# First two columns of each weight group run abreast in the scan stage of a two-layer encoder

## Chip, cores and metric

One Trainium2 chip, one core. The metric is the device time of one execution in microseconds. TensorE is called PE here, VectorE DVE, ScalarE ACT, GpSimd POOL and SyncE SP, as in the profile.

## The reference

Two token sequences of 512 x 1024 (s = 0 and s = 1) go through the same two layers. Layer 0 is an RWKV-7 mixer that scans forward and backward; layer 1 is attention in a 2-D neighbourhood.

```python
def _rwkv7_branch(xn, mu, w_r, w_k, w_v, w_z, ...):
    ...
    lerp = lambda j: xn + xx * mu[j]
    r = heads(lerp(0) @ w_r)
    k = heads(lerp(1) @ w_k)
    v = heads(lerp(2) @ w_v)
    z = xn @ w_z
    ...
    for d in range(2):
        ...                       # decay, a, k_d by two small products each
        ys.append(_wkv7_scan(r, decay, k_d, v, -kk, kk * a, reverse=(d == 1)))
    ...                           # y: sum of both, normed by head, plus a bonus
    return (y * silu(z)) @ w_o

def _natten_branch(xn, w_in, b_in, rpb, w_o, b_o):
    q, k, v, z = jnp.split(xn @ w_in + b_in, 4, axis=-1)
    ...                           # windowed softmax attention with a bias
    return (o * silu(z)) @ w_o + b_o

def _trunk(x, ...):
    for i in range(2):
        h = branch_i(_rms_norm(x, pre_norm_g[i]))
        x = x + _rms_norm(h, post_norm_g[i])
    return x
```

## The kernel before

**Products.** Every large product is split in two halves of lower precision: an fp32 block becomes a high half (`hi`, an ACT cast, lines 745 for weights and 771 for inputs) and a low half (`lo`, a DVE subtraction, lines 747 and 773). A *column* is one 128-wide slice of outputs for all 512 tokens: eight blocks of channels (k = 0 to 7), and for each a *triple* of matmuls (lines 826 to 828: hi x hi, hi x lo, lo x hi), all added up in one PSUM bank (`pm`). The weights of a column come in two halves of 512 columns (`raw`, `whi`, `wlo`; three raw buffers, four split ones).

**Stages.** `prelude` (to about 170 us) norms the inputs and makes the first columns. `scan_phase` (to about 1170 us) runs the scan of all heads, and beside it 80 columns. `rest` does the attention; its columns are made by `gemm` (lines 430 to 432).

**The scan stage.** Eight pairs of heads' blocks (four for each sequence) go through `prep` (lora products, lines 896 and 897, with `th` on ACT, line 900), `inverse` (elimination on DVE, lines 1018 and 1020, between transposes at lines 1011, 1028 and 1033; then four takes of a `pm` bank, copied by lines 1056 and 1059), eight `step`s each (lines 1186 to 1254), and `finish` (lines 1279 to 1317), which writes y. PSUM has three `pm` banks in this stage, one `us`, and two each of `pf` and `zy`.

**The columns beside it.** They come in groups that share one input: group 0 is w_r of s = 0, 1 w_v of s = 0, 2 w_k, 3 w_r, 4 w_v of s = 1 (8 columns each), 5 six columns of w_z of s = 1, 6 w_o of s = 0 (8, whose input is y of the first four finishes), 7 the other two of w_z, and 8 the first 24 columns of w_in of s = 0. At most nine pairs of input halves fit (`NACT` = 18), so a block of the next group can only be made when the last column of the group before has used one up. `flow` (line 722) holds the generators: `loads` and `splits` for weights, `fetched` and `operands` for inputs, `products` for the triples, and `posts` for what follows a column (its *end*: copy, activation, store, for v also two transposes that take a `pm` bank each). In group 8 inputs are made by `residual`, `scaled` and `squares`, and the ends wait for the norm of that input, which takes `pm` banks in `rstds`.

**The order** of PE, DVE and ACT in this stage is fixed when the kernel is built. `weave` (line 1617 on) keeps a clock model and asks generators (*threads*) for what they can do next; each has a rank, and the lowest that can start goes first. PE work goes only when no other engine's does. Steps have rank 0, `prep` 1.5, ends 2, `operands` 2.5, `splits` 3 or 9 (9 when more than one split half is in stock), `inverse` 5, `products` 9. Where the model finds nothing for PE and the clock might drop, it puts a warming matmul (line 1643) into a spare part of the `zy` bank. `inverse` is one thread: it takes the eight one after another.

Before the change a column runs k = 0 to 7 before the next begins, and two threads of ends take columns in turn: `posts(0)` the even ones, `posts(1)` the odd ones.

Of the kernel before, what the change touches and what calls it, by code (L numbers as in the profile page):

```python
# [19 lines left out]
P = 128  # L20
T = 512
D = 1024
KT = D // P
NP = 8
NCH = 8
# [25 lines left out]
class Clock:  # L51
# [40 lines left out]
    def room(self, key, bufs):  # L92
        s = self.slots.get(key, ())
        return 0.0 if len(s) < bufs else min(self.left(n) for n in s)
# [137 lines left out]
class Trunk:  # L232
# [9 lines left out]
    TOK = True  # L242
    LAST = ("pg", "pg", "po", "pm")
    PG, PT, NK, NPT = 2, 2, 2, 3
    AHEAD, AHEADW, SCAN_A, SCAN_W = 0, 0, 300, 300
    NAB, NX, NR, NY, NSB, NBI = 2, 2, 2, 2, 4, 2
    NAK, NZ = 1, 1
# [25 lines left out]
    def name(self, s):  # L273
        self.uid += 1
        return f"{s}_{self.uid}"
# [356 lines left out]
    def column(self, s, kind, p, ps):  # L632

        nc, sp = self.nc, self.sp
        vt, act = nc.vector, nc.scalar
        first = lambda e: (e, None, lambda c, n=ps.tensor.name: c.at([n]))
        keep, whole = self.clock.keep, ps.tensor.name
        if kind == "z":

            o, th = self.tmp(), self.tmp()  # L640
            if s == 0:
                yield first("D")
                vt.tensor_tensor(o, ps, self.rstd0, op=ALU.mult)
                ps = o
            yield "A" if s == 0 else first("A")
            keep.add(whole)
            act.activation(th, ps, AF.Tanh, scale=0.5)
            yield "D"
            keep.discard(whole)
            vt.scalar_tensor_tensor(o, th, 1.0, ps, op0=ALU.add, op1=ALU.mult)  # L650
            self.save("z", s, p, o)
            return
        yield "A", None, lambda c: max(c.at([ps.tensor.name]), min(c.room(("tmp", id(self.main)), self.NTMP), 1e10))
        o = self.tmp()
        if kind == "k":
            keep.add(whole)
        act.copy(o, ps)
        self.save(kind, s, p, o)
        if kind == "r":
            self.made.add((kind, s, p))  # L660
            return
        if kind == "k":
            yield "A"
            keep.discard(whole)
            sq = self.tmp()
            act.activation(sq, ps, AF.Square, scale=self.vec("kk", p))
            free, room = self.bank()
            yield "P", free, lambda c: max(room(c), c.at([sq.tensor.name]))
            ss = self.p("pm", (2, T))
            nc.tensor.matmul(ss, self.ssel, sq, start=True, stop=True)  # L670
            yield "A"
            row = self.tmp((2, T))
            act.copy(row, ss)
            if p == 0:
                sp["ss", s] = self.dram(f"ss{s}", (16, T))
            self.load(sp["ss", s][2 * p:2 * p + 2], row)
            self.made.add((kind, s, p))
            if p == NP - 1:
                yield "S", None, lambda c: c.at([sp["ss", s].tensor.name])

                rn = self.tmp((P, 64))
                self.load(rn, sp["ss", s].rearrange("a (b c) -> (a b) c", b=8))
                yield "A"
                act.activation(rn, rn, AF.Sqrt)
                yield "D"
                vt.tensor_scalar(rn, rn, 1e-12, None, op0=ALU.max)
                vt.reciprocal(rn, rn)
                sp["rn", s, 0] = self.dram(f"rn{s}", (16, T))
                self.load(sp["rn", s, 0].rearrange("a (b c) -> (a b) c", b=8), rn)
                self.made.add(("rn", s))  # L690
            return

        if p == 0:

            sp["vt", s] = self.dram(f"vt{s}", (4, 2, NCH // 2, 2, L, 2, 2, HD))
        yield "A"
        back = self.tmp()
# [14 lines left out]
        self.made.add((kind, s, p))  # L712
# [9 lines left out]
    def flow(self):  # L722


        nc, did, ck = self.nc, self.did, self.clock
# [5 lines left out]
        for k, t in enumerate(self.groups[0][1]):  # L731
            x[0, k] = t

        def loads():
            for c, (_, _, src, _) in enumerate(cols):
                for j in range(2):
                    yield "S", lambda: did["load"] < did["split"] + self.NRAW
                    raw[2 * c + j] = self.load(self.t("raw", (P, self.WP), self.NRAW), src[:, j * self.WP:(j + 1) * self.WP])
                    did["load"] += 1

        def splits():
            for h in range(2 * len(cols)):
                yield "A", lambda: h < did["load"] and h < did["k"] // 4 + self.NW, lambda c: c.at(name(raw[h]))
                hi, lo = (self.t(tag, (P, self.WP), self.NW, F32R) for tag in ("whi", "wlo"))
                nc.scalar.copy(hi, raw[h])  # L745
                yield "D"
                nc.vector.tensor_tensor(lo, raw.pop(h), hi.bitcast(F32), op=ALU.subtract)  # L747
                w[h] = hi, lo
                did["split"] += 1
# [63 lines left out]

        def products():
            free, room = self.bank()
            for c, (g, j, _, done) in enumerate(cols):
                for k in range(KT):
                    h = 2 * c + k // 4
                    at = slice(k % 4 * P, k % 4 * P + P)
                    yield (  # L820
                        "P", lambda: h in w and (g, k) in x and (k > 0 or (free() and c - 2 not in self.post)),
                        lambda c: max(c.at(name(*w[h], *x[g, k])), 0.0 if k else room(c)))
                    if k == 0:
                        ps = self.p("pm")
                    (hi, lo), (xh, xl) = w[h], x[g, k]
                    nc.tensor.matmul(ps, hi[:, at], xh, start=(k == 0), stop=False)  # L826
                    nc.tensor.matmul(ps, hi[:, at], xl, start=False, stop=False)  # L827
                    nc.tensor.matmul(ps, lo[:, at], xh, start=False, stop=(k == KT - 1))  # L828
                    did["k"] += 1
                    if j == len(self.groups[g][2]) - 1:  # L830
                        did["x"] += 1
                self.post[c] = done(ps)

        def posts(a):
            for c in range(a, len(cols), 2):
                yield "A", lambda: c in self.post
                yield from self.post[c]
                del self.post[c]
# [2 lines left out]
        return [  # L841
            Thread(lambda: 0, loads()), Thread(lambda: 3 if few() else 9, splits()), Thread(lambda: 0, fetched()), Thread(lambda: 2.5, operands()),
            Thread(lambda: 0.6, residual()), Thread(lambda: 0.6, scaled()), Thread(lambda: 0.6, squares()),
            Thread(lambda: 9, products()), Thread(lambda: 2, posts(0)), Thread(lambda: 2, posts(1))]


    def prep(self, s, p):
# [479 lines left out]
    def out0s(self, s, p, ps):  # L1327

        nc = self.nc
# [12 lines left out]
        else:  # L1342
# [1 line left out]
            nc.scalar.activation(sq, h, AF.Square)  # L1344
            yield "D"
            nc.vector.tensor_tensor(self.h_acc, sq, self.h_acc, op=ALU.add)
        if p == NP - 1:
            self.made.add(("h", s))

    def out0(self, s):  # L1350
# [307 lines left out]
    def scan_phase(self, mid):  # L1658
# [27 lines left out]
        def fetch():  # L1686
            for q in qs:
                st = self.steps[q]
                yield (
                    "S", lambda: did["states"] >= q - 1 and did["preps"] > st.n and ("v", st.s, 2 * st.pb + 1) in self.made,  # L1690
                    lambda c: c.at([self.sp["ab", st.s, st.pb].tensor.name]))
                self.fetch(st)
                did["fetch"] += 1
# [19 lines left out]

        def finish():
            for n, (s, pb) in enumerate(self.todo):
                yield "S", lambda: did["steps"] >= NCH * (n + 1) and ("z", s, 2 * pb + 1) in self.sp
                yield from self.finish(s, pb, self.steps[NCH * n].y)
                did["finish"] += 1

# [212 lines left out]
```

## Time and profile before

| | |
|---|---|
| time, median of 3 runs | 1655.09 us (1649.51 to 1655.29) |
| profiled execution | 1656.04 us, its span 1654.2 us |
| granted PE clock, mean | 0.977 |
| busy in the span | PE 94%, DVE 74%, ACT 61%, POOL 11% |
| scan stage | 170 to 1170 us of the span |
| prelude, `rest` | 0 to 170 us, 1170 to 1654.2 us |

Inversions, by the start of line 1011 on DVE and of the last copy (line 1059, an ACT pair of 1.2 us), and the first column of the groups, from its first triple to its end; all in us:

| inversion | starts | last copies | group | first column |
|---|---|---|---|---|
| 0 | 242.1 | 322.4 | 1 | 230.8 to 246.4 |
| 1 | 323.2 | 430.3 | 2 | 328.0 to 349.6 |
| 2 | 431.1 | 545.5 | 3 | 446.2 to 466.0 |
| 3 | 546.3 | 657.4 | 4 | 530.0 to 544.0 |
| 4 | 656.2 | 762.1 | 5 | 642.2 to 658.9 |
| 5 | 762.1 | 895.0 | 6 | 742.4 to 767.4 |
| 6 | 895.5 | 1021.4 | 7 | 850.2 to 871.7 |
| 7 | 1021.4 | 1092.0 | 8 | 877.0 to 921.6 |

The page gives each engine's busy time as a share of the span; a group's row gives its line, engine, operation and tiles, the count, then busy time in us and the mean of one in ns, then the idle time before it and what ended that. A row of the timeline gives the start, the time taken, and in brackets the idle time before it. A row of the windows gives the window, its length, and for each engine the busy time and the count.

### The profile page before, as it was taken

What the parts mean: (1) busy time and instruction counts of PE and PEld (TensorE: products, weight loads), DVE (VectorE), ACT (ScalarE), POOL (GpSimd) and SP (SyncE); (2) the same over time, 40 slices, a digit from 0 to 9 for tenths busy, and PEclk for the clock granted to TensorE, in tenths of its full rate; (3) what the DMA queues carried; (4) which work ended last, traced back from release to release, by engine and by line L of the source; (5) the groups of instructions that cost most, each with busy time, mean ns of one, the idle gap of its engine ahead of it and who ended that gap; (6) DMA issues with size and microseconds to landing.
All of it is one profiled execution on the core that took longest, in us unless ns stands there. A gap on an engine that the chain in (4) does not pass through costs nothing.

```text
span 1654.2 us, 46534 instructions
## 1 busy us (share of the span) xinstructions
PE 1558.4 (94%) x18826; PEld 1195.2 (72%) x18826; DVE 1220.0 (74%) x2711; ACT 1014.5 (61%) x2027; POOL 178.2 (11%) x338
## 2 busy tenths in 40 slices
PE   7989899898989998999888999999999999999998
PEld 6867667676767776766666777777777788777776
DVE  8886669588778786897788897855576685665564
ACT  6577655766755767566475665454567665455562
POOL 0000213311101133100000011000000002100000
PEclk9989999899999999999997999999999999999999
DMA  6455678666677687675776674554864346745553
GB/s 212 158 176 185 183 270 279 217 227 227 206 246 255 201 279 261 201 252 165 226 229 225 199 255 166 179 190 127 276 222 164 109 140 213 244 157 175 169 159 107
DMA packets 176184, 336.29 MB, mean 203 GB/s; under 512 B 20928, under 2 KB 53824, under 8 KB 175968
## 3 DMA queue, kind: packets, MB, share of 16 engines
q1 hardware_dynamic: 152480, 253.07, 47.7%
q0 software_dynamic: 23488, 80.23, 13.8%
q8 instruction: 148, 2.42, 0.6%
q14 instruction: 68, 0.56, 0.1%
HBM read 227.71 MB, written 105.51 MB: 201 GB/s over the span
## 4 chain that ended last, share of the span: by engine, by line
PE 48%; DVE 7%; ACT 5%; DMA 3%; issue 3%; POOL 0%; SPq 0%; DVEq 0%; ACTq 0%; POOLq 0%
PE pg L430 6%; PE pg L431 6%; PE pg L432 6%; PE pm L826 4%; PE pm L827 3%; PE pm L828 3%; PE pf L1114 2%; PE sc L1452 2%; PE po L1485 2%; PE pt L1470 2%; PE us L1233 1%; PE zy L1186 1%; PE us L1213 1%; PE zy L1237 1%; DMA v<-dv 1%
## 5 line engine op out<-in xcount | busy, mean ns | idle before, releaser
L826 PE MATMUL pm<-act,whi 128*128 128x512 f32 x640 | 283.9, 444 | 7.8 <-ACT act L795 3.2
L827 PE MATMUL pm<-act,whi 128*128 128x512 f32 x640 | 257.2, 402 | 10.8 <-DVE act L773 10.1
L828 PE MATMUL pm<-act,wlo 128*128 128x512 f32 x640 | 256.2, 400 | 5.5 <-DVE wlo L747 5.5
L430 PE MATMUL pg<-act,whi 128*128 128x512 f32 x384 | 158.4, 412 | 0.4 <-DVE tmp L1408 0.4
L826 PEld LDWEIGHTS pm<-act,whi 128*128 128x128 f32 x640 | 121.7, 190 | 50.9 <-issue 10.7
L379 ACT CAST whi<-raw 128x512 fp32r<-128x512 f32 x148 | 91.4, 617 | 107.7 <-PE pg L431 66.1
L432 PE MATMUL pg<-act,wlo 128*128 128x512 f32 x384 | 152.5, 397 | 0.0
L431 PE MATMUL pg<-act,whi 128*128 128x512 f32 x384 | 152.4, 397 | 0.0
L827 PEld LDWEIGHTS pm<-act,whi 128*128 128x128 f32 x640 | 122.8, 192 | 36.7 <-DVE act L773 15.9
L828 PEld LDWEIGHTS pm<-act,wlo 128*128 128x128 f32 x640 | 122.7, 192 | 35.5 <-DVE wlo L747 8.9
L380 DVE TENSOR_TENSOR wlo<-raw,whi 128x512 fp32r<-128x512 f32 x148 | 101.3, 686 | 61.1 <-ACT whi L379 60.3
L747 DVE TENSOR_TENSOR wlo<-raw,whi 128x512 fp32r<-128x512 f32 x160 | 108.9, 683 | 33.3 <-ACT whi L745 33.1
L745 ACT CAST whi<-raw 128x512 fp32r<-128x512 f32 x160 | 97.8, 617 | 44.6 <-PE pm L827 23.3
L430 PEld LDWEIGHTS pg<-act,whi 128*128 128x128 f32 x384 | 72.2, 188 | 15.5 <-issue 3.3
L432 PEld LDWEIGHTS pg<-act,wlo 128*128 128x128 f32 x384 | 72.2, 188 | 14.9 <-issue 0.3
L431 PEld LDWEIGHTS pg<-act,whi 128*128 128x128 f32 x384 | 72.4, 189 | 14.1 <-issue 2.5
L1018 DVE TENSOR_TENSOR etmp<-N 128x30 f32<-128x30 f32 (+14 forms) x240 | 78.4, 327 | 4.3
L1020 DVE TENSOR_TENSOR N<-etmp,N 128x30 f32<-128x30 f32 (+14 forms) x240 | 78.5, 327 | 4.0
L1463 DVE CUSTOM_DVE_ANT_0 sb<-sc,bias 128x256 f32<-128x256 f32 x128 | 49.2, 418 | 26.2 <-PE pt L1470 20.1
L1466 ACT ACTIVATE sb<-sb,mx 128x256 f32<-128x256 f32 x128 | 64.1, 502 | 6.9 <-DVE mx L1465 6.6
L1114 PE MATMUL pf<-cab 64*64 64x128 f32 (+1 forms) x2048 | 67.0, 268 | 0.3 <-PE zy L1092 0.3
L1137 DVE TENSOR_TENSOR AK<-zy,cc 128x256 f32<-128x256 f32 x63 | 26.6, 422 | 53.0 <-PE zy L1092 52.5
(409 smaller groups left out, 3686.8 us busy)
## 6 DMA issues: line engine op xcount, KB each, us to landing
dab<-ab POOLq DMA_DIRECT2D x32, 1024.0 KB, 7.0
cab<-dab SPq DMA_DIRECT2D x64, 512.0 KB, 5.0
raw<-in_w_in_dram SPq DMA_DIRECT2D x128, 256.0 KB, 2.9
bias<-in_rpb_dram SPq DMA_DIRECT2D x32, 384.0 KB, 5.2
raw<-in_w_z_dram SPq DMA_DIRECT2D x32, 256.0 KB, 3.6
raw<-in_w_k_dram SPq DMA_DIRECT2D x32, 256.0 KB, 3.0
raw<-in_w_r_dram SPq DMA_DIRECT2D x32, 256.0 KB, 4.2
k<-dk SPq DMA_DIRECT2D x32, 256.0 KB, 4.6
```

The costliest lines, as they stand in the source:

```text
L379: self.nc.scalar.copy(hi, src)
L380: (eng or self.nc.vector).tensor_tensor(lo, src, hi.bitcast(F32), op=ALU.subtract)
L430: nc.tensor.matmul(ps, hi, x[k][0], start=(k == 0), stop=False)
L431: nc.tensor.matmul(ps, hi, x[k][1], start=False, stop=False)
L432: self.mm = nc.tensor.matmul(ps, lo, x[k][0], start=False, stop=(k == KT - 1))
L745: nc.scalar.copy(hi, raw[h])
L747: nc.vector.tensor_tensor(lo, raw.pop(h), hi.bitcast(F32), op=ALU.subtract)
L826: nc.tensor.matmul(ps, hi[:, at], xh, start=(k == 0), stop=False)
L827: nc.tensor.matmul(ps, hi[:, at], xl, start=False, stop=False)
L828: nc.tensor.matmul(ps, lo[:, at], xh, start=False, stop=(k == KT - 1))
L1020: vt.tensor_tensor(N[:, q + 1:, :q], tv, N[:, q + 1:, :q], op=ALU.add)
L1114: end = nc.tensor.matmul(st.f[half(a), h, 0, d, g] if st.last else st.f[half(a), h, :, d, g], ab[half(h), d, g, 2 * e[d] + 1 - a], rt if s ...
```

## The change

For the groups in `PAIRS` (1 to 8) the first two columns run abreast: triple k of the first, then triple k of the second, for k = 0 to 7. `ENDS` would do the same with a group's last two columns; it is empty. The list `turns` holds the order of (column, block), `halves` the order in which weight halves are needed; `loads` and `splits` follow it, and a split half's buffer is free again when its four triples are done (`used`). During a pair two `pm` banks are filled at once. The ends run in three threads, so a column may start while the ends of the two before it are pending. Since ends may now finish in another order, the guards that looked for the last or the second of some columns look for all of them.

```diff
+    PAIRS, ENDS = (1,2,3,4,5,6,7,8), ()
...
             if p == NP - 1:
-                yield "S", None, lambda c: c.at([sp["ss", s].tensor.name])
+                yield "S", lambda: all(("k", s, q) in self.made for q in range(NP)), lambda c: c.at([sp["ss", s].tensor.name])
...
+        turns = []
+        for c, (g, j, _, _) in enumerate(cols):
+            n = len(self.groups[g][2])
+            two = [a for a, gs in ((0, self.PAIRS), (n - 2, self.ENDS)) if g in gs]
+            if j in two:
+                turns += [(c + e, k) for k in range(KT) for e in range(2)]
+            elif j - 1 not in two:
+                turns += [(c, k) for k in range(KT)]
+        halves = [2 * c + k // 4 for c, k in turns if k % 4 == 0]
+        used = Counter()
...
         def loads():
-            for c, (_, _, src, _) in enumerate(cols):
-                for j in range(2):
+            for h in halves:
...
         def splits():
-            for h in range(2 * len(cols)):
-                yield "A", lambda: h < did["load"] and h < did["k"] // 4 + self.NW, lambda c: c.at(name(raw[h]))
+            for n, h in enumerate(halves):
+                yield "A", lambda: n < did["load"] and (n < self.NW or used[halves[n - self.NW]] == 4), lambda c: c.at(name(raw[h]))
...
         def products():
-            for c, (g, j, _, done) in enumerate(cols):
-                for k in range(KT):
...
-                        "P", lambda: h in w and (g, k) in x and (k > 0 or (free() and c - 2 not in self.post)),
+            for c, k in turns:
...
+                    "P", lambda: h in w and (g, k) in x and (k > 0 or (free() and c - 3 not in self.post)),
...
-                    if k == 0:
-                        ps = self.p("pm")
+                if k == 0:
+                    out[c] = self.p("pm")
+                ps = out[c]
...
         def posts(a):
-            for c in range(a, len(cols), 2):
+            for c in range(a, len(cols), 3):
...
-            Thread(lambda: 9, products()), Thread(lambda: 2, posts(0)), Thread(lambda: 2, posts(1))]
+            Thread(lambda: 9, products()), *(Thread(lambda: 2, posts(a)) for a in range(3))]
...
-        if p == NP - 1:
+        self.did["h", s] += 1
+        if self.did["h", s] == NP:
             self.made.add(("h", s))
```
In `fetch` and `finish` of `scan_phase` the tests for v and z of block 2 * pb + 1 become tests for both blocks of the pair.

More of the change, by code (lines that the diff above doesn't have):

```diff
@@ L732, in flow @@
             x[0, k] = t
-        def loads():
-            for c, (_, _, src, _) in enumerate(cols):
-                for j in range(2):
-                    yield "S", lambda: did["load"] < did["split"] + self.NRAW
-                    raw[2 * c + j] = self.load(self.t("raw", (P, self.WP), self.NRAW), src[:, j * self.WP:(j + 1) * self.WP])
-                    did["load"] += 1
+        turns = []
[7 more added lines that the diff above has]
+        halves = [2 * c + k // 4 for c, k in turns if k % 4 == 0]
+        place = {h: n for n, h in enumerate(halves)}
+        used = Counter()
+        def loads():
+            for h in halves:
+                yield "S", lambda: did["load"] < did["split"] + self.NRAW
+                j = h % 2
+                raw[h] = self.load(self.t("raw", (P, self.WP), self.NRAW), cols[h // 2][2][:, j * self.WP:(j + 1) * self.WP])
+                did["load"] += 1
         def splits():
-            for h in range(2 * len(cols)):
-                yield "A", lambda: h < did["load"] and h < did["k"] // 4 + self.NW, lambda c: c.at(name(raw[h]))
+            for n, h in enumerate(halves):
+                yield "A", lambda: n < did["load"] and (n < self.NW or used[halves[n - self.NW]] == 4), lambda c: c.at(name(raw[h]))
                 hi, lo = (self.t(tag, (P, self.WP), self.NW, F32R) for tag in ("whi", "wlo"))
@@ L815, in products @@
             free, room = self.bank()
-            for c, (g, j, _, done) in enumerate(cols):
-                for k in range(KT):
-                    h = 2 * c + k // 4
-                    at = slice(k % 4 * P, k % 4 * P + P)
-                    yield (
-                        "P", lambda: h in w and (g, k) in x and (k > 0 or (free() and c - 2 not in self.post)),
-                        lambda c: max(c.at(name(*w[h], *x[g, k])), 0.0 if k else room(c)))
-                    if k == 0:
-                        ps = self.p("pm")
[L825 to L832, printed above, removed]
+            out = {}
+            for c, k in turns:
+                g, j, _, done = cols[c]
+                h = 2 * c + k // 4
+                at = slice(k % 4 * P, k % 4 * P + P)
+                yield (
+                    "P", lambda: h in w and (g, k) in x and (k > 0 or (free() and c - 3 not in self.post)),
+                    lambda c: max(c.at(name(*w[h], *x[g, k])), 0.0 if k else room(c)))
+                if k == 0:
+                    out[c] = self.p("pm")
+                ps = out[c]
+                (hi, lo), (xh, xl) = w[h], x[g, k]
+                nc.tensor.matmul(ps, hi[:, at], xh, start=(k == 0), stop=False)
+                nc.tensor.matmul(ps, hi[:, at], xl, start=False, stop=False)
+                nc.tensor.matmul(ps, lo[:, at], xh, start=False, stop=(k == KT - 1))
+                did["k"] += 1
+                used[h] += 1
+                if j == len(self.groups[g][2]) - 1:
+                    did["x"] += 1
+                if k == KT - 1:
+                    self.post[c] = done(out.pop(c))
         def posts(a):
-            for c in range(a, len(cols), 2):
+            for c in range(a, len(cols), 3):
                 yield "A", lambda: c in self.post
@@ L1689, in fetch @@
                 yield (
-                    "S", lambda: did["states"] >= q - 1 and did["preps"] > st.n and ("v", st.s, 2 * st.pb + 1) in self.made,
+                    "S", lambda: did["states"] >= q - 1 and did["preps"] > st.n and all(("v", st.s, 2 * st.pb + g) in self.made for g in range(2)),
                     lambda c: c.at([self.sp["ab", st.s, st.pb].tensor.name]))
@@ L1715, in finish @@
             for n, (s, pb) in enumerate(self.todo):
-                yield "S", lambda: did["steps"] >= NCH * (n + 1) and ("z", s, 2 * pb + 1) in self.sp
+                yield "S", lambda: did["steps"] >= NCH * (n + 1) and all(("z", s, 2 * pb + g) in self.sp for g in range(2))
                 yield from self.finish(s, pb, self.steps[NCH * n].y)
```

## The prediction

> **What bounds the kernel now.** I read the page first, then the stages, then the scan stage alone: its groups, its waits, the windows of the first columns, and last the order of the slowest chain in it.
>
> ```profile
> span 1654.2 us, 46534 instructions
> ...
> PE 1558.4 (94%) x18826; PEld 1195.2 (72%) x18826; DVE 1220.0 (74%) x2711; ACT 1014.5 (61%) x2027; POOL 178.2 (11%) x338
> ```
> ```profile
> 170.00:1170.00 1000.00, 931.19 (x15480) 705.71 (x15479) 779.07 (x1496) 621.39 (x1205) 146.47 (x239) 0.97 0.68 219
> ```
> The scan stage is the 1000 us from 170 to 1170 (the row's columns: PE, PEld, DVE, ACT, POOL, granted clock, DMA share, GB/s). PE stands idle for 69 us of it. Some busy time is not work either: the groups of that window, ahead of the waits of PE, hold the warming matmuls of line 1643, which the planner puts where it finds nothing to run.
>
> ```profile
> L1643 PE MATMUL zy<-cc 128*128 128x256 f32 x190 | 51.7, 402 | 1.0 <-ACT Z L1198 0.5 <-ACT y L1252 0.5
> ```
> ```profile
> PE pm L827 <- DVE act L773: 10.1, 11, 4.7
> ```
> So about 69 + 52 = 121 us of PE time in the stage carry no work, and PE's largest wait by one releaser is for the low half of an input block (`act`, line 773). Those are the blocks of a new group. The timeline of PE at the start of w_o shows one such start, three triples (lines 826 to 828) in 9 us:
>
> ```profile
> 742.35 0.58 PE L826 MATMUL pm<-act,whi 128*128 128x512 f32 x1
> 747.59 0.80 PE L827 MATMUL pm<-act,whi 128*128 128x512 f32 x1 [4.66 <-DVE act L773]
> 748.18 0.63 PE L828 MATMUL pm<-act,wlo 128*128 128x512 f32 x1
> 748.61 2.53 PE L1643 MATMUL zy<-cc 128*128 128x256 f32 x6
> 750.79 0.58 PE L826 MATMUL pm<-act,whi 128*128 128x512 f32 x1
> ```
> But PE is not what paces the stage. The eight inversions (lines 1011 to 1059) do, one after another. Below are the first line of an inversion, then for two of them the last copy of the one before on ACT and the first transpose of the next on DVE, and the last copy of all:
>
> ```profile
> L1011 DVE STREAM_TRANSPOSE N<-Gd x8: 1937/2004/2054, 242.1 to 1021.4; 128x1024 f32<-128x1024 f32 x8
> ```
> ```profile
> 545.52 1.18 ACT L1059 COPY MT<-pm 32x512 f32<-32x512 f32 x2
> ```
> ```profile
> 546.26 2.02 DVE L1011 STREAM_TRANSPOSE N<-Gd 128x1024 f32<-128x1024 f32 x1
> ```
> ```profile
> 1021.43 1.18 ACT L1059 COPY MT<-pm 32x512 f32<-32x512 f32 x2 [0.67 <-PE pm L1051]
> ```
> ```profile
> 1021.40 2.05 DVE L1011 STREAM_TRANSPOSE N<-Gd 128x1024 f32<-128x1024 f32 x1
> ```
> ```profile
> 1092.04 1.18 ACT L1059 COPY MT<-pm 32x512 f32<-32x512 f32 x2 [1.68 <-PE pm L1051]
> ```
> Each begins within about 2 us of the end of the last (all eight are in the table of the profile section), from 242.1 to 1093.2: 851 us without a pause. They run on what DVE has left: in the eight stretches of elimination (from line 1011 to line 1022) DVE is busy 549.87 of 646 us, 85%.
>
> ```profile
> sum 646.00, PE 606.77 PEld 461.10 DVE 549.87 ACT 400.79 POOL 78.99; mean PE 75.85 PEld 57.64 DVE 68.73 ACT 50.10 POOL 9.87
> ```
> After the last inversion come eight steps of the scan (the last product of line 1237 at 1142.07), then the last finish (line 1317, to 1165.1 and 0.75 more). The column stream ends beside it at 1160.5, and `rest`'s first columns (line 430) already slip in between:
>
> ```profile
> 1142.07 0.70 PE L1237 MATMUL zy<-X,R 128*64 128x64 f32 x16
> ...
> 1151.18 0.40 PE L430 MATMUL pg<-act,whi 128*128 128x512 f32 x1
> ...
> 1160.09 0.39 PE L828 MATMUL pm<-act,wlo 128*128 128x512 f32 x1
> ```
> ```profile
> L1317 DVE SCALAR_TENSOR_TENSOR sz<-bv,dv,sz x16: 700/751/753, 405.3 to 1165.1; 128x512 f32<-128x512 f32 x16
> ```
> Two things end the stage together, then: the chain of inversions, steps and finish at 1166, the columns at 1160.5.
>
> **The change, part by part.** No matmul, load or copy is added or taken away; their order changes. What it can win is idle PE time in the first column of a group, since the second column then has a triple for each block that arrives. A column whose blocks are all there takes 5.6 us (the second of group 1, first and last matmul):
>
> ```profile
> 246.24 0.39 PE L826 MATMUL pm<-act,whi 128*128 128x512 f32 x1
> ...
> 251.48 0.39 PE L828 MATMUL pm<-act,wlo 128*128 128x512 f32 x1
> ```
> So a group can win at most 5.6 us, and at most its idle time. The windows run from a first column's first block to its end. For groups 1 to 5 all instructions, then line 1643 alone:
>
> ```profile
> sum 87.70, PE 77.81 PEld 55.27 DVE 68.38 ACT 58.87 POOL 16.08; mean PE 15.56 PEld 11.05 DVE 13.68 ACT 11.77 POOL 3.22
> ```
> ```profile
> sum 87.70, PE 7.86 PEld 5.52; mean PE 1.57 PEld 1.10
> ```
> That is 9.9 idle and 7.9 of warming, 17.8 us at most. I count it at nothing, because the stream then stops for something else: group 5 ends at 723.8, and the next, w_o, needs y of the fourth finish. In the stretch 723.8 to 742.4 PE warms for 11.13 us:
>
> ```profile
> 723.80:742.40 18.60, 11.13 (x50) 8.98 (x49) 1.00 0.83 263
> ```
> Columns that end earlier only lengthen that wait, unless the inversions before it end earlier too; DVE has the same work up to that point. If y came earlier, the 17.8 would count in full.
>
> Groups 6 to 8 (w_o, the rest of z, w_in); the rows are those of group 7, which has the least idle time of the three, and of group 8, all instructions; then group 7 in line 1643 alone:
>
> ```profile
> 850.20:871.70 21.50, 15.58 (x73) 11.76 (x62) 18.86 (x41) 10.69 (x21) 1.45 (x2) 0.84 0.92 299
> 877.00:921.60 44.60, 37.32 (x829) 27.43 (x832) 35.93 (x60) 28.57 (x55) 2.43 (x3) 0.81 0.64 214
> ```
> ```profile
> 850.20:871.70 21.50, 2.86 (x10) 2.10 (x10) 0.84 0.92 299
> ```
> Group 7 has 5.9 + 2.9 = 8.8 us without work, above 5.6, so all three count in full: 3 x 5.6 = 16.8 us. The stream would end at 1143.7 in place of 1160.5. The chain beside it still ends at 1166, and only `rest`'s columns can move into the room. Bounds: 0, if none does, and 16.8, if all of it is filled. The row at 1151.18 shows that they do slip in, the one at 1160.09 that they take a part; I take half, 8.4 us.
>
> Against it stands DVE. Three columns' worth of work ahead of the inversions is three times two weight splits, and I put a column's end at one more such instruction:
>
> ```profile
> L747 DVE TENSOR_TENSOR wlo<-raw,whi 128x512 fp32r<-128x512 f32 x157 | 106.8, 683 | 31.7 <-ACT whi L745 31.5
> ```
> 3 x 3 x 0.683 = 6.1 us. Elimination is 646 of the 851 us, so 0.76 of it, 4.7 us, falls in front of one; bounds 0 and 6.1.
>
> **Weights.** At a group's start two halves must be split in place of one, and with four buffers two are ahead instead of three. The loads on SP go in the same new order, none is added, and the splits' gate counts the same halves. I put it at nothing; the bound is one split late for a group that counts, 3 x 0.683 = 2 us. **Ends.** Three threads let the third column start while two ends are pending; counted in the bank rival below. The guards with `all` wait for the later of two in place of the last: nothing. The planner lays the whole stage out anew, so that other neighbours change as well; that has no sign, and it stands in the range.
>
> Sum: -8.4 + 4.7 = -3.7. The profiled execution took 1656.04 us, 1.84 of it outside its span, and lies 1 us above the median of 1655.09; I leave that 1 us. 1656 - 4 = **1652**. Half a per cent, 8 us, is about what a measurement of this kernel can tell from no change.
>
> **The rivals.** *PE is the bound after all.* From 877 on the columns fill every gap, and if the chain gives way as they end sooner, 16.8 us are won in full: 1656 - 17 = 1639. If the low clock of groups 7 and 8 goes too, that is 21.5 x 0.16 + 44.6 x 0.19 = 11.9 us of lost pulses more, to 1627. For it: 121 us without work, and a stage in which columns and chain end 5 us apart. Against it: the unbroken row of inversions. 0.34.
>
> *The banks.* The stage has three `pm` banks. A pair holds two, from its first block until its ends have read them; before, a column held one, and its end another for a short time. What is left is one bank for the inversion (four takes each, one after another), prep, the transposes behind v and finish. Prep's hold of a bank is lines 896, 897 and then 900 on ACT:
>
> ```profile
> L896 PE MATMUL pm<-h,w2h 128*128 128x512 f32 x64 | 28.7, 449 | 1.1 <-ACT tmp L673 0.4 <-ACT vs L476 0.3 <-ACT NA L1056 0.3
> ```
> ```profile
> L900 ACT ACTIVATE th<-pm,dv 128x512 f32<-128x512 f32 x64 | 43.9, 685 | 7.8 <-PE pm L897 7.5
> ```
> With line 897 taken like 896 that is 0.45 + 0.45 + 0.69 = 1.6 us; four takes that each wait for one make 6.4 us for an inversion. The inversion that ends at 546.7 (above) does so while group 4's first columns run, and so does this one with group 5's:
>
> ```profile
> 657.36 1.18 ACT L1059 COPY MT<-pm 32x512 f32<-32x512 f32 x2 [1.83 <-PE pm L1051]
> ```
> By the table of the profile section two more end inside a first column, in groups 6 and 8. If half of the four collide, the chain grows by 13 us and nothing of the gain is seen: 1656 + 13 = 1669. It decides from the point where an inversion's copies lie over 4 us further apart than now. For it: this is the unbroken chain. Against it: the planner gives prep and inversion a bank before a product. 0.25.
>
> *The clock.* Triples that change banks one by one might leave gaps that cost clock: 16 columns x 5.6 = 90 us of matmuls at 0.81, the lowest clock above, are 21 us more: 1677. Against it speaks a stretch in which the columns already alternate with the scan's tiles:
>
> ```profile
> 970.00:1070.00 100.00, 98.49 (x1718) 75.80 (x1720) 81.66 (x179) 51.83 (x101) 10.34 (x17) 1.00 0.55 184
> ```
> 0.03. The Trainium skill, "TensorE: Matmul & The Clock Gate", section "A second HAM failure mode: psum-queue depth-cycling", says that cycling through PSUM banks at each iteration makes PE idle for moments, often enough for the clock to swing between half and full; by that rule this rival would come. The trace does not agree so far: 1.00 in the row above.
>
> *Abreast only by name.* If the second column's weights come late each time, its triples gather behind the first's, as now: 1656. 0.03.
>
> **How the numbers follow.** Forecast 0.35 and the last rival 0.03 lie within half a per cent: 0.38. Faster is the first rival, 0.34; slower banks and clock, 0.28. The likeliest case alone reaches from 1656 - 16.8 + 4.7 = 1644 to 1656 + 6 + 2 = 1664. The range goes on into the two large rivals: down to 1634, inside the first one's 1627 to 1639, and up to 1670, past the banks' 1669.
>
> **What would show it.** Right: warming and idle PE time in the three last first-column windows down by 15 us; the wait before w_o longer; inversions still end to start, the last copy near 1093; line 430 earlier before the stage's end. The first rival: the last inversion ends over 8 us sooner. The banks: inversions whose copies lie further apart. Wrong in the root: a chain of inversions that moves by more than 8 us either way.

## The result and the profile after

The change takes 1662.58 us (median of 10 runs) against 1654.38 for the kernel before in the same runs: a ratio of 1.0044, 95% interval 1.0030 to 1.0057, so 8.2 us slower where 3 us faster were forecast. The profiled execution has a span of 1661.7 us, 7.5 more than before, at the same work:

```profile
span 1661.7 us, 46524 instructions
...
PE 1555.9 (94%) x18830; PEld 1192.7 (72%) x18830; DVE 1220.9 (73%) x2711; ACT 1011.9 (61%) x2025; POOL 177.9 (11%) x338
```
The scan stage now lasts to about 1177.5. Its window, then the warming matmuls in it (line 1661 now):

```profile
170.00:1177.50 1007.50, 929.42 (x15490) 704.01 (x15489) 780.30 (x1498) 619.50 (x1205) 146.40 (x241) 0.97 0.68 218
```
```profile
L1661 PE MATMUL zy<-cc 128*128 128x256 f32 x194 | 49.0, 391 | 0.0
```
PE idles for 78.1 us and warms for 49.0: 127 us without work, against 121 before. PE's waits for the low half of a block made by `operands` (line 786 now) were 10.1 us and are 2.1. But PE now waits once, for 8.2 us, for the high half of a block (line 784): for the first of w_o. Together that is 10.3 us, as before (10.1 and 0.2):

```profile
PE pm L842 <- DVE act L786: 2.1, 2, 2.0
PE pm L841 <- ACT act L784: 8.2, 1, 8.2
```
The whole loss is there when the last inversion ends, at 1100.3 in place of 1093.2 (ACT's timeline, line 1076 now):

```profile
1099.15 1.18 ACT L1076 COPY MT<-pm 32x512 f32<-32x512 f32 x2 [0.29 <-PE pm L1068]
```
From there to the end of the span it is 561.4 us, and 561.0 before. So the question is why the stretch from the first inversion to the last grew. The same two rows of the windows, before and then after, from the start of line 1011 (1028) to that last copy; the third pair of numbers is DVE:

```profile
242.10:1093.20 851.10, 791.63 (x13744) 599.73 (x13743) 692.24 (x1360) 541.54 (x1051) 127.25 (x207) 0.97 0.69 224
```
```profile
243.40:1100.30 856.90, 787.78 (x13741) 595.68 (x13741) 693.45 (x1361) 539.61 (x1050) 127.05 (x207) 0.97 0.69 223
```
DVE does the same work in both, 692 and 693 us; the stretch is longer by 5.8 us, of which DVE's idle time is 4.6 (158.9 to 163.5). The rest of the 7.1 is a later start, by 1.3.

The delay does not build up evenly. Against the table of the kernel before, the inversions 0 to 7 start 1.3, 2.5, 7.9, 5.3, 8.1, 20.9, 17.0 and 7.0 us later. So 21 us are lost by the start of inversion 5, 13 of them in inversion 4, which starts beside the pair of group 5, and 14 are won back beside groups 6 to 8.

**Where PE's time went.** In the first two columns of groups 6 to 8 the change does what it says. The last line (the sum) of the windows of the first columns before, all instructions and line 1643 alone, then the same for the pairs after, with the row of group 8's pair ahead, 759.3 to 784.3, 867.3 to 880.0 and 885.2 to 924.1:

```profile
sum 91.10, PE 72.82 PEld 53.69 DVE 72.70 ACT 51.14 POOL 6.34; mean PE 24.27 PEld 17.90 DVE 24.23 ACT 17.05 POOL 2.11
...
sum 91.10, PE 12.09 PEld 7.78; mean PE 4.03 PEld 2.59
```
```profile
885.20:924.10 38.90, 32.73 (x577) 23.83 (x578) 34.88 (x59) 24.75 (x44) 1.89 (x2) 1.00 0.69 222
sum 76.60, PE 68.26 PEld 51.13 DVE 65.01 ACT 44.20 POOL 5.81; mean PE 22.75 PEld 17.04 DVE 21.67 ACT 14.73 POOL 1.94
...
sum 76.60, PE 9.28 PEld 7.55; mean PE 3.09 PEld 2.52
```
Without work: 18.3 + 12.1 = 30.4 us before, 8.3 + 9.3 = 17.6 after. But PE waits longer ahead of these groups. The stretches from a group's end to the next one's first triple, before (723.8 to 742.4 and 848.8 to 850.2; none ahead of group 8) and after (741.0 to 759.3, 858.1 to 867.3, 880.0 to 885.2), in the same order:

```profile
sum 20.00, PE 16.83 PEld 13.57 DVE 18.70 ACT 15.34 POOL 2.57; mean PE 8.41 PEld 6.79 DVE 9.35 ACT 7.67 POOL 1.29
...
sum 20.00, PE 11.13 PEld 8.98; mean PE 5.56 PEld 4.49
```
```profile
sum 32.70, PE 20.32 PEld 15.88 DVE 26.39 ACT 18.95 POOL 4.31; mean PE 6.77 PEld 5.29 DVE 8.80 ACT 6.32 POOL 1.44
...
sum 32.70, PE 11.55 PEld 9.29; mean PE 3.85 PEld 3.10
```
That is 14.3 us before and 23.9 after. Of the 12.8 won, 9.6 are given back at once. At the start of w_o it is not y that is late: the fourth finish ends at 748.4, the loads of the first three blocks were issued at 646.0 to 649.2, and the first triple still comes only at 759.3. The cast of the first block (line 784) stands in ACT's fixed order behind an activation of prep, this one waits for DVE, and DVE waits for a store of prep (DVE's timeline, then ACT's):

```profile
755.75 0.69 DVE L957 TENSOR_TENSOR ab<-r,e 128x512 f32<-128x512 f32 x1 [5.05 <-DMA dab<-ab]
```
```profile
757.93 0.81 ACT L969 ACTIVATE pp<-th,dv 128x512 f32<-128x512 f32 x1 [6.50 <-DVE ab L957]
758.65 1.12 ACT L784 CAST act<-xr 128x512 fp32r<-128x512 f32 x2
```
In the kernel before, the first triple came 1.1 us after the end of the fourth finish (741.3), here 10.9 us after it.

**The stuck pair.** The largest single loss is group 5. Before, from the end of group 4 to the end of its second column (637.5 to 674.9), PE had 3.9 us idle and 2.1 of warming; after, in the pair's window, 7.6 and 10.4:

```profile
637.50:674.90 37.40, 33.55 (x689) 24.95 (x692) 26.56 (x48) 27.61 (x59) 8.36 (x14) 0.91 0.80 266
```
```profile
629.50:690.60 61.10, 53.51 (x1030) 40.28 (x1029) 43.01 (x79) 41.79 (x81) 12.10 (x19) 0.89 0.66 215
...
629.50:690.60 61.10, 10.35 (x36) 7.44 (x36) 0.89 0.66 215
```
PE's timeline shows why. Line 841 begins a triple; the others write a `pm` bank too, but for the inversion (lines 1066, 1068), prep (913), the transposes of v (705) and finish (1319):

```profile
629.46 0.40 PE L841 MATMUL pm<-act,whi 128*128 128x512 f32 x1
...
630.67 1.20 PE L1066 MATMUL pm<-NA,Go 32*32 32x32 f32 x64
...
636.05 0.50 PE L913 MATMUL pm<-h,w2h 128*128 128x512 f32 x1 [2.25 <-ACT NA L1073]
...
640.69 1.97 PE L705 MATMUL pm<-cc,tmp 128*128 128x128 f32 x8 [0.78 <-ACT th L917]
...
646.87 1.02 PE L1319 MATMUL pm<-ks,cc 128*128 128x512 f32 x2
...
652.70 1.20 PE L1066 MATMUL pm<-NA,Go 32*32 32x32 f32 x64
...
656.01 0.76 PE L1068 MATMUL pm<-MT,NA 32*32 32x32 f32 x36 [2.11 <-ACT NA L1073]
...
658.87 0.80 PE L841 MATMUL pm<-act,whi 128*128 128x512 f32 x1 [0.80 <-DVE bv L1332]
```
The first column takes a bank at 629.46. The second column's first triple comes at 658.87. Its weights were split by 630.1 and three input blocks were made by 629.6 (DVE's timeline):

```profile
628.88 0.66 DVE L786 TENSOR_TENSOR act<-xr,act 128x512 fp32r<-128x512 f32 x1
629.44 0.70 DVE L760 TENSOR_TENSOR wlo<-raw,whi 128x512 fp32r<-128x512 f32 x1
```
Two things hold the second column for these 29 us. The first is the gate: it may start only when the end three columns back, that of the seventh column of w_v, is done. The first transposes of that end fill a bank by 628.9, but the copy out of it comes at 640.54 in ACT's order, and its second copy at 642.15 or later. So until then the gate is shut, and one bank more is held:

```profile
640.54 0.58 ACT L708 COPY vs<-pm 128x512 f32<-128x512 f32 x1
...
642.15 0.59 ACT L708 COPY vs<-pm 128x512 f32<-128x512 f32 x1
```
The second, for the 16 us that are left, is the bank: all others go first at the two that remain, `products` having the last rank. Because the order in a pair is fixed, the first column's blocks 1 and 2, which are ready and have their bank, stand behind the second column. That is a wait that one column at a time cannot have.

### The profile page after: what moved, and what is told of

Same layout as the page of the kernel before. It is cut to its first block, busy times and chain, and to the rows that moved or that the text cites. A ratio compares the mean times of both kernels' runs of the same rounds, so it can differ in the third digit from the quotient of the medians.

```text
span 1661.7 us, 46524 instructions
## 1 busy us (share of the span) xinstructions
PE 1555.9 (94%) x18830; PEld 1192.7 (72%) x18830; DVE 1220.9 (73%) x2711; ACT 1011.9 (61%) x2025; POOL 177.9 (11%) x338
## 4 chain that ended last, share of the span: by engine, by line
PE 66%; DVE 12%; ACT 11%; DMA 6%; issue 5%; SPq 0%; DVEq 0%; POOL 0%; ACTq 0%; POOLq 0%
PE pm L841 6%; PE pg L431 6%; PE pg L432 6%; PE pg L433 6%; PE pm L843 5%; PE pm L842 5%; PE pf L1131 3%; PE us L1250 2%; PE sc L1470 2%; PE zy L1203 2%; DMA dab<-ab 2%; PE us L1230 2%; PE po L1503 2%; PE zy L1254 2%; PE pt L1488 2%
## 5 line engine op out<-in xcount | busy, mean ns | idle before, releaser
L1242 ACT COPY X<-us 64x256 f32<-64x256 f32 x128 | 46.8, 366 | 38.5 <-PE zy L1109 34.9
```

## The experiments

Three theories stood at the start. *Banks*: a pair, or a third pending end, takes `pm` banks from the inversion and prep. *Third thread*: the three threads of ends with their wider gate (a column may start while two ends are pending, not one) are the loss by themselves. *Replanning*: any new order of this stage moves its end by some us. Each ratio is against the kernel before in the same runs. Where "last inversion" stands, it is the end of its last copy in the one profiled execution, which can lie some us off the median.

**The two halves of the change.** First the ends alone (`threads_only`), then the pairs alone.

```diff
-    PAIRS, ENDS = (1,2,3,4,5,6,7,8), ()
+    PAIRS, ENDS = (), ()
```


> The change with PAIRS empty: columns one by one as before, but ends in three threads and the gate of a column's start two ends back instead of one. Theory banks (a pair holds two of three pm banks and so delays the inversions' takes): no pair, so as before, 1654 within 3 us, last inversion ends near 1093. Theory third thread (three pending ends crowd ACT and the banks): all of the loss, 1662, last inversion near 1100. Theory replanning (any change of the order moves the chain of inversions by some us without a sign): anywhere from 1646 to 1665.

1665.52 us, ratio 1.0066 (1.0050 to 1.0082), last inversion 1105.4.

```diff
-    ... free() and c - 3 not in self.post ...
+    ... free() and c - 2 not in self.post ...
-            for c in range(a, len(cols), 3):
+            for c in range(a, len(cols), 2):
...                                    # and two threads
```


> The change with its pairs, but ends in two threads and the old gate (a column starts when the end two columns back is done). Theory banks: the loss stays, 1660 to 1665, first-column waits for act below 5 us as in the change. Theory third thread: the loss goes, 1650 to 1655. Theory replanning: anywhere from 1646 to 1668.

1662.47 us, ratio 1.0055 (1.0034 to 1.0075), last inversion 1105.5. Each half alone is as slow as both together, so neither theory that blames one half holds: without pairs there should have been no loss for theory banks, without the third thread none for theory third thread. The losses do not add, either. And in `pairs_two_threads` PE's waits for blocks made by `operands` do fall, to 3.1 us in all, with no gain in time.

**A bank held, with no pair.**

```diff
+                    if g and j == k == 0:
+                        yield "P", free, room
+                        hold = self.p("pm")
+                        nc.tensor.matmul(hold[:, 0:64], self.ident, self.scan[0][:, 0:64], start=True, stop=True)
...                                    # read by ACT after the group's second column
```


> The kernel before with one more pm bank held from the first triple of each of groups 1 to 8 to the end of the group's second column, by a matmul of 64 columns into it and an ACT copy of one column out of it (8 of each, under 4 us of work in all). No column runs abreast. Theory banks: the price without the gain, 1662 or more, inversions' copies further apart. Theories third thread and DVE (columns that come earlier put their weight splits ahead of eliminations): 1654 to 1657, the last inversion within 2 us of 1093.

1679.33 us, ratio 1.0146 (1.0121 to 1.0171). The time is as theory banks had it, but its other sign is missing: the inversions' copies (from the first of line 1056 to the last of line 1059) lie 104 us apart in sum, 102 before. And this is one layout; see those below. 22 us of it are a wait of inversion 4 for prep. DVE's work up to the last inversion is the same again, 697 us, and its idle time 179:

```profile
241.90:1117.50 875.60, 808.24 (x13788) 609.56 (x13787) 696.57 (x1366) 543.33 (x1060) 127.65 (x208) 0.96 0.68 220
```

**The pair unstuck.** The second column joins only when a bank is free; until then the first goes on alone.

```diff
-            for c, k in turns:
+            # next: of the pair's columns that can go, the one whose operands are there first
+            ok = [c for c in cs if can(c) and (c == cs[0] or at_k[c] < at_k[cs[0]])]
+            return min(ok, key=lambda c: (when(c, clock), at_k[c])) if ok else None
```


> The change, but the second column of a pair takes its bank only when one is free, and until then the first column goes on alone; three threads of ends and the wide gate stay. Theory stuck pair (at the start of group 5 the second column's first triple waits 29 us for a bank and holds all products up): the 18 us of idle and warming PE time in that pair's window fall below 9, the time by 2 to 8 us to 1655 to 1660. Theory third thread (columns and pending ends hold all three banks): most of the loss stays, above 1660. Theory replanning: no sign.

1660.26 us, ratio 1.0033 (1.0017 to 1.0049). In group 5's pair PE now has 7.4 us idle and 4.0 of warming, 11.4 in place of 17.9:

```profile
629.20:674.10 44.90, 37.49 (x578) 27.73 (x578) 31.69 (x50) 32.03 (x59) 10.52 (x16) 0.85 0.75 253
...
629.20:674.10 44.90, 3.98 (x14) 2.66 (x14) 0.85 0.75 253
```
The pair is shorter by 16 us, but less was won there than expected (below 9 us), and the two ratios' intervals overlap. Inversion 5 begins 10 us earlier than in the change (772.9 for 783.0) and the last inversion ends at 1095.7, so the pair may have cost some us; that it cost time at the end is not shown.

The same with two threads of ends:

> As flex_three, but with two threads of ends and the old gate. Theory banks as a whole: both causes are gone, the first columns' idle time is filled and the time is 1655 or less; the last inversion at 1093 or before. Theory replanning: within 6 us of 1655, without a sign.

1666.04 us, ratio 1.0079 (1.0060 to 1.0098), last inversion 1107.2. With both supposed causes gone it should have been 1655 or less. Theory banks, as a sum of these two parts, falls.

**The inversion first at the banks.**

```diff
-            ... Thread(lambda: 5, inverse()), Thread(lambda: 1.5, preps()),
+            ... Thread(lambda: 0.4 if self.tail else 5, inverse()), Thread(lambda: 1.5, preps()),
```


> The change, with the inversion's thread at rank 0.4 in place of 5 from its copies after elimination to its end, so that it goes ahead of prep, ends, finish and products for its four banks and copies. Theory banks (the chain of inversions is held up where it asks for banks): the sum of the eight stretches from the end of elimination to the last copy, 220 us in the change, falls by 40 or more, and the time with it, by 5 to 30 us. Theory DVE alone (the chain is paced by what DVE leaves to elimination, and a shorter stretch is taken back there or in prep): under 4 us.

1693.21 us, ratio 1.0239 (1.0215 to 1.0262), the other way from all theories. The stretches from elimination (line 1022, 1039 in the change) to the last copy did shrink, from 220 to 173 us in all, but inversions now waited for prep, 65 us in all, which they hardly did in the change (4 us):

```profile
243.30:1126.10 882.80, 801.46 (x13798) 608.75 (x13797) 696.17 (x1365) 541.64 (x1054) 128.00 (x209) 0.97 0.67 218
```
DVE: 696 us of work, 187 idle. For the kernel before:

> The kernel before with the same rank. Theory banks: it gains less than the change does, since a bank more is free (215 us in those stretches before): 0 to 15 us. Theory DVE alone: under 4 us.

1657.53 us, ratio 1.0021 (1.0008 to 1.0034): none of the gain that theory banks had possible. Its stretches shrank too, from 215 to 178 us, and it waited 35 us for prep, where before it waited for none. So the inversions are not a chain of their own. An inversion starts when the one before it and its own prep are both done, and that prep runs beside the inversion before it, on the same engines and banks: in these two runs, what the inversion gained the prep lost.

**Neutral new layouts.** `EPS` and `NEAR` are slacks of the planner, 60 and 400 ns (by how much an instruction may be late and still count as able to start, and how early the last products of a step may queue), and have nothing to do with the change. Two theories are left, and the expectations name them so: *scatter*, which is replanning (any new layout moves the time), and *own cost* (the change costs by itself).

> The kernel before with the planner's slack EPS at 55 instead of 60 ns: nothing of the change, the order laid out anew. Theory replanning: the last inversion ends 3 to 10 us from 1093, either way, and the time with it. The other theories: 1654 within 2 us.

> The kernel before, EPS at 65 ns: a second neutral new layout (the first, 55 ns, gave 1652). Theory replanning (8 us are within what any new layout does): 5 us or more away from 1654, either way. Theory that the change costs by itself: within 4 us of 1654, as at 55.

> The kernel before, EPS at 57 ns: a third neutral layout. Theory scatter: anywhere from 1650 to 1672. Theory own cost: within 5 us of 1654.

> The kernel before, NEAR (how early the planner lets the step's last products queue) at 390 in place of 400 ns: a neutral layout by another parameter. Theory scatter: anywhere from 1650 to 1672, and above 1654 more likely than below, because the kernel before is one layout that came out well. Theory own cost: within 5 us of 1654.

> The change, EPS at 50 ns. Theory that the change costs by itself: 1659 to 1668, whatever the layout. Theory replanning: it may as well lie below 1655.

> The change, EPS at 57 ns. Theory scatter: anywhere from 1650 to 1672, so that it may lie below a layout of the kernel before. Theory own cost: 1659 to 1668.

> The change, NEAR at 390 ns. Theory scatter: anywhere from 1650 to 1672. Theory own cost: 1659 to 1668.

| kernel | slack | us | ratio (95%) | last inversion | DVE idle to there |
|---|---|---|---|---|---|
| before | as it is | 1654.4 | 1 | 1093.2 | 158.9 |
| before | NEAR 390 | 1653.95 | 0.9985 (0.9970 to 1.0000) | 1092.2 | 156.2 |
| before | EPS 55 | 1652.06 | 0.9996 (0.9979 to 1.0014) | 1097.5 | 161.7 |
| before | EPS 65 | 1670.07 | 1.0080 (1.0061 to 1.0100) | 1109.9 | 168.3 |
| before | EPS 57 | 1688.74 | 1.0211 (1.0173 to 1.0248) | 1118.9 | 175.6 |
| change | as it is | 1662.58 | 1.0044 (1.0030 to 1.0057) | 1100.3 | 163.5 |
| change | NEAR 390 | 1660.99 | 1.0043 (1.0016 to 1.0071) | 1103.7 | 167.0 |
| change | EPS 50 | 1662.73 | 1.0044 (1.0028 to 1.0060) | 1107.5 | 173.3 |
| change | EPS 57 | 1666.45 | 1.0078 (1.0056 to 1.0100) | 1108.2 | 171.6 |

The last two columns are those of the profiled execution; with EPS 55 this took 1658.35 us, 6 more than the median. Three nanoseconds of slack move the kernel before by 2.1%, almost five times the change's effect, and the four layouts of the change lie inside the five of the kernel before. Theory scatter was right that neutral layouts differ by more than the change, but it missed EPS 55, which was to move by 3 to 10 us and didn't, and it put the upper end at 1672, 17 us below EPS 57. Theory own cost missed two layouts of the kernel before (EPS 65 and 57), but all three further layouts of the change lie in its band of 1659 to 1668. In the slowest layout, inversion 3 ends at 632.3, but inversion 4 cannot begin before prep does its last step (line 991) at 675.7; it begins at 676.0. ACT's and then DVE's timeline of that kernel:

```profile
631.09 1.18 ACT L1059 COPY MT<-pm 32x512 f32<-32x512 f32 x2 [2.68 <-PE pm L1051]
```
```profile
674.97 0.75 DVE L991 SCALAR_TENSOR_TENSOR kp<-kp,cv,r 128x512 f32<-128x512 f32 x1
...
675.97 1.93 DVE L1011 STREAM_TRANSPOSE N<-Gd 128x1024 f32<-128x1024 f32 x1
```
43.7 us of waits like that one stand in this layout and none in the kernel before, whose prep is done 0.8 us before the second inversion begins (line 991 ends at 322.4, line 1011 starts at 323.2) and stays ahead from there. But EPS 65, 0.8% slower than the kernel before, has only 1.7 us of such waits, so they are not what all slow layouts share. NEAR 390 keeps nearly the whole order (596 triples begun before the last inversion ends, in both) and the time; so does the change at NEAR 390 (595 in both). That leaves four distinct layouts of the kernel before, two at 1652 to 1654 and two slower, and three of the change.

**Only the pairs that could win.**

```diff
-    PAIRS, ENDS = (1,2,3,4,5,6,7,8), ()
+    PAIRS, ENDS = (6,7,8), ()
```


> The change with pairs in groups 6 to 8 alone (three threads and the wide gate stay). The forecast's account, in which only these three groups can win: 1650 to 1656. Theory third thread: as with no pairs at all (1665), 1662 to 1668. Theory pairs cost banks wherever they are: between 1660 and 1665, like the others.

1666.72 us, ratio 1.0075 (1.0047 to 1.0103), no better than no pairs (1665.52). In this one layout the forecast's account of the gain, taken by itself, is not borne out.

**Columns with fewer banks.**

```diff
-                        "P", lambda: ... free() and c - 2 not in self.post)),
+                        "P", lambda: ... free() and c - 1 not in self.post)),
```


> The kernel before, where a column starts only when the end of the column just before it is done (gate one column back): columns and ends hold one pm bank instead of up to two. Theory banks (what prep, inversion and finish lack is banks): the idle time of DVE up to the last inversion, 159 us before, falls below 150 and the time below 1650. Theory PE (columns that start late cost PE time that is then missing): 1658 or more, with more idle and warming time between columns.

1763.78 us, ratio 1.0659 (1.0635 to 1.0683): the one effect far outside the scatter. The last inversion ends at 1041.5, 52 us sooner than before, and the last column at 1271.6, 111 us later:

```profile
241.50:1041.50 800.00, 703.44 (x13334) 534.06 (x13333) 623.06 (x1239) 479.54 (x947) 116.95 (x188) 0.95 0.65 207
```
DVE's work up to there is 623 us in place of 692, since the columns that were held back need it later. Its idle time is 177 us, not below 150, and the kernel is slower, so theory banks missed both its numbers; theory PE had the time right. What the run shows is that columns held back let the inversions run sooner, by tens of us, and through DVE. Whether the bank that is set free has a part in it beside the later columns, this run doesn't separate.

## Why the prediction was wrong

The forecast was 1652, the measured time lies 8 us above the kernel before: the sign was wrong. The step that failed is the term that the sum put at nothing, the new layout ("that has no sign, and it stands in the range"), and with it the chain that was to stay, its last copy near 1093, while the columns won 8.4 us. Measured, the columns ended 7.2 us later, not 16.8 sooner, the last copy came 7.1 us later, and new layouts that change nothing else cost from nothing to 35 us. By its steps:

- *What bounds the stage.* That PE's idle time alone does not set the time was right: `pairs_two_threads` cut PE's waits for input and won nothing. That the row of inversions paces the stage was half right: in all profiles but the one with fewer banks for columns the span ends 556 to 566 us after the last inversion, while that moves by 34 us (1092.2 to 1126.1). But "without a pause" was a property of this one layout. Prep was 0.8 us from holding up the second inversion, and I took the slack for a law. A row was misread, too: the start of w_o shows two triples in 9 us, not three.
- *Groups 1 to 5 count nothing.* The first two columns of groups 1 to 4 had 17.5 us without work and have 8.7, and the stream still stopped for 18.3 us ahead of group 6 (18.6 before). That it stopped for y was not so in the change (above). Wrong in sign for group 5, which lost 12 us.
- *Groups 6 to 8 win 16.8 us.* They won 12.8 in their windows, and gave back 9.6 ahead of them. The stream was to end at 1143.7; its last triple ended at 1167.7, since the groups began 17, 17 and 8 us later than before. This step failed: a window of idle time is only worth something if what stands around it comes earlier as well, and I looked at each window by itself.
- *DVE against it, 4.7 us.* Didn't occur: 595 triples were begun when the last inversion ended, and 596 before, and DVE had worked 693 and 692 us.
- *Weights at nothing.* PE's waits for split halves are 8.3 us in place of 7.8: nothing speaks against it.
- *The rival of the banks.* Its sign came, its price did not follow from it. The inversions' copies lie 117 us apart in sum, 14.6 more than before; 17.8 of that is inversion 3, beside the stuck pair, while inversion 0 has 12.8 less. But the time doesn't go with it: in `pairs_two_threads` the copies lie 100 us apart and the last inversion ends at 1105.5, in `flex_three` 113 us and 1095.7. The experiments give banks no size of their own in the change.
- *The clock* stayed: 0.979 against 0.977. In the windows of the eight pairs it was 0.89 to 1.00, where the same columns one by one had 0.84 to 1.00. The rule of the Trainium skill, "TensorE: Matmul & The Clock Gate", section "A second HAM failure mode: psum-queue depth-cycling" (cycling through banks at each iteration makes the clock swing), is not what this trace shows, though banks alternate from triple to triple there.
- *The new layout.* This is the term that was mis-sized. It got no number. For the kernel before, three distinct new layouts cost nothing, 13 and 35 us, and the change's 8 us lie inside that.

What stays open is the cause of these 8 us: scatter of the layout is large enough for them, but that it is the whole cause isn't shown. The four layouts of the change lie 0.43 to 0.78% above the kernel before, and the five kernels with a part of the change or the unstuck pair lie 0.33 to 0.79% above it, while two of the four distinct layouts without it lie at 1652 to 1654. The other two are at 1670 and 1689, so the change may cost by itself, or the kernel before may be a layout that came out well. To settle it one would need many more neutral layouts of both kernels, or a change of the pairs' order alone with all other instructions in place; neither was tried.

## What to carry to other kernels

Before costing a reordering in a kernel whose order a greedy planner lays out, move one of the planner's slacks by a few per cent and time that: if it moves the kernel more than the change does, the change's effect can't be read from one pair of kernels. An engine's idle time in a window is a gain only if what follows in that stream does not wait for something else, be it only its place in another engine's fixed order. And where two streams of work share a small pool of buffers, a fixed order inside the stream of lowest rank lets one missing buffer hold up work that already has its own.

## What the runs showed that I had not expected

From the first inversion to the last DVE did 691 to 700 us of work in every layout but that of the fewer banks, while the stretch ranged from 849 to 883 us: the layouts differ mainly in idle time. And a gate that lets a column start only when the end just before it is done moved 69 us of DVE work across that point, and the last inversion 52 us forward, at a price of 6.6% of the whole time.
